# Two orders in a hybrid decoder kernel: DMAs of two groups issued alternately, evictions of product sums handed out unit by unit

## The chip, the core and the metric

The kernel runs on one core of one Trainium2 chip. The core has five engines with an instruction queue each: TensorE (PE in the profile, with PEld for its weight loads), VectorE (DVE), ScalarE (ACT), GpSimd (POOL) and SyncE (SP, which here only issues DMAs). Matmuls write their sums to PSUM, in eight banks; everything else works in SBUF. An engine runs its queue strictly in order and waits on semaphores for the others. The metric is the time of one execution on the device in microseconds; before the change it is 2410.54 us, the median of three runs (2407.71 to 2413.61).

## The reference

One layer of a decoder over a prompt of 2048 tokens and 64 sample tokens, model width 1024, all in float32:

```python
proj = x @ w_in                       # q | f | i | g | B | C | h
o, state = hgrn2(silu(q), log_f, 1 - f, i)          # gated linear recurrence, 4 heads of 128
o = rms_norm(o) * onorm_g * silu(g)
yc = B * conv3(C * h)                 # causal, depthwise
x = layer_norm(ALPHA * x + concat(o, yc) @ w_out)
x = layer_norm(ALPHA * x + relu(x @ w_ff1) ** 2 @ w_ff2)    # w_ff1 1024 x 4096, w_ff2 4096 x 1024
```

It returns the rows of both groups, and the new states of the recurrence and of the convolution.

## The kernel before

**Blocks and stages.** The prompt is worked in four blocks of 512 tokens (`b`); the 64 sample tokens go with the second. A block runs through the input projection (`m1`, `m2`, `m3`, together `main()`), the recurrence (`head`, `chunks`, `out_stages`), the output projection with the first normalisation, the first MLP matmul (`ff1`, `ff1_product`) and the second (the loop over `ff2_units`). The order of all instructions is written out by hand: generators yield between pieces and the loop at line 862 interleaves them, and each engine's queue is simply the order in which the Python code emits.

**Split numbers.** Every float32 operand of the large matmuls is split in a high and a low part, and a product is three matmuls (`mm3`, lines 239 to 241, and `mm3_on`, 245 to 247): high by high, high by low, low by high. For weights ACT makes the high part `wh` (line 203) and DVE the low part `wl` (line 210); for activations `split` makes `h` on ACT (line 164) and `l` on DVE (line 165).

**The weights' pipeline.** All weights are a list of units of 128 x 1024 values. SP loads each to one of three buffers `st` (line 182), ACT and DVE split it into one of four `wh` and four `wl`. `weights(u)` calls `ahead`, which keeps four units split ahead of the one that PE works on. DVE's part of a step is not emitted at once: it goes on the list `later`, and the next `flush()` emits that list, in order. `ahead` begins with such a flush, so what one unit puts on `later` is emitted as the next unit begins.

**Products with fewer multiplications.** Most of the MLP runs as Strassen-like products: seven in place of eight for a chunk of the hidden width (`PRODUCTS`). Some of these take sums of quarters of the weights. The sums are made once, in DRAM: `T1` to `T4` for each of eight chunks, for `w_ff2` in tensors named `T_b` (`quarter2`) and for `w_ff1` in tensors named `T_a` (`quarter1`). `make_sums` (line 341) is a generator that issues these as DMAs from POOL: it goes through eight steps (copy or accumulate), and in each through its chunks, one DMA of 512 KB per `yield`. A step on a chunk reads or adds to what an earlier step on the same chunk has written, so POOL waits for that DMA to land before it issues. `making` (line 356) first makes the `T_b` sums of chunks 0 to 3 and then the `T_a` sums of chunks 4 to 7, 32 DMAs each. In the first block, from the seventh piece of `main()` on, lines 868 and 869 take two DMAs of it per piece; `hold` (line 351) is a tiny POOL operation that keeps POOL from starting earlier. Further sums come from `making1` during the MLP. POOL also computes the powers of the normalisations: line 720 for the recurrence's output, line 271 for the layer norms.

**The recurrence's output.** `out_stages` (line 711) squares and sums a chunk's heads on ACT (716), adds a constant on DVE (719), takes the power on POOL (720), scales on ACT (723), multiplies by the gate on DVE (725), transposes on PE (729) and splits. Each stage is emitted in a step of its own, between pieces of the projection.

**The second MLP matmul.** A block has two passes (`pl["parts"]`), each over four chunks (three in the last pass of the last block, whose eighth chunk is done apart). A pass runs through the seven products in order, and each product through its chunks: 28 units, each 12 matmuls of 512 columns. A product's sum stands in two PSUM banks (128 rows each): bank pair `D` takes `T4`, `A` takes `B11`, then `T2`, then `T3` on top, `C` takes `B21`, `B` takes `T1` and then `B22`. After a product's last chunk (`c == clast`) the sums are added to rows of the output `x1` in SBUF by `add_to` (line 1238), one DVE operation on 128 x 512 values for each bank and target: two for most products, four for `T3`. The first addition to a target is line 1245, the others are line 1242. These are the evictions. Line 1234, by way of `sum_rows`, makes sums of hidden rows for three of the products; `prepare` splits the hidden rows of the unit two ahead (`h`, `l`). In the second block `sample_sums` adds the sample rows' two half sums (lines 256 and 1252) at once and puts the additions to the output on the list `slow`; each unit moves one entry of `slow` to `later` (line 1307), and what is left is emitted as the pass ends (line 1345).

Of the kernel before, what the change touches and what calls it, by code (L numbers as in the profile page):

```python
# [34 lines left out]
NCH = NF // FC  # L35
# [19 lines left out]
NPART = 4  # L55
# [6 lines left out]
def hybrid_step(ctx, tc, a, o):  # L62
# [45 lines left out]
    def PS(shape=(P, 512)):  # L108
        count[0] += 1
        return psum.tile(list(shape), F32, tag="ps", bufs=8, name=f"ps{count[0]}")  # L110
# [42 lines left out]
    later = []  # L153

    def flush():
        for _ in range(len(later)):
            later.pop(0)()

    def flush_all():
        while later:  # L160
            flush()
# [64 lines left out]
    def weights(i, kept=0):  # L226

        ahead(i + 4 - kept)
        return handles.pop(i)
# [23 lines left out]
    def upper(bank):  # L253

        tmp = TMP().rearrange("p a b -> p (a b)")
        s.activation(tmp[:NS], bank[NS:2 * NS, :], AF.Copy)
        return tmp[:NS]


    def norm_weights(which, rows=range(2)):  # L260

        for i in rows:
            nc.sync.dma_start(lnb[:, i, :], a["lnb"][:, 2 * which + i, :])
# [78 lines left out]
    def make_sums(at, cs):  # L342
        for to, of, acc in (("T1", "B11", False), ("T3", "B22", False), ("T1", "B12", True), ("T3", "B12", True),
                            ("T2", "T3", False), ("T2", "B11", True), ("T4", "T2", False), ("T4", "B21", True)):
            for c in cs:
                if acc:
                    g.dma_start(at(c, to), at(c, of), accum_op=ALU.add, max_dma_last_dim=4096)
                else:
                    g.dma_start(at(c, to), at(c, of), max_dma_last_dim=4096)
                yield  # L350

    def hold(x):

        g.tensor_tensor(tick, x, x, ALU.add)

    making = chain(make_sums(quarter2, range(NPART)), make_sums(quarter1, range(NPART, NCH)))
    making1 = chain(make_sums(quarter2, range(NPART, NCH)), make_sums(quarter1, range(NPLAIN, NPART)))

    for b in range(NB):
# [44 lines left out]
    for b in range(NB):  # L404
# [542 lines left out]
        def drain():  # L947
            while lnq:
                before()
                after()  # L950
                flush()
# [31 lines left out]
        for ps_i, tl in enumerate(pl["tiles"]):  # L983
# [5 lines left out]
            banks = {(t, dh): PS() for t in tl for dh in range(2)}  # L989
# [45 lines left out]
        def values(c):  # L1035
            if c not in raw:

                raw[c] = F((P, 4, 2, 256), "raw", NPART)
            return raw[c]
# [170 lines left out]
        def prepare():  # L1210
            if not queue:
                return
            step, c = queue.pop(0)
            r = raw[c]
            x = r[:, SLOT_OF[step]]
            h, l = F((P, 2, 256), "h", 3, F32R), F((P, 2, 256), "l", 3, F32R)
            split(h, l, x)
            hid[step, c] = (h, l)
            if step in SUMMED:
                assert (step, c) in summed  # L1220
            seen.add((step, c))
            if step == PRODUCTS[-1][0]:
                del raw[c]
# [14 lines left out]
        def add_to(t, dh, bank, sign):  # L1238
            z = x1[t][:, dh * 512:dh * 512 + 512]
            op = ALU.add if sign > 0 else ALU.subtract  # L1240
            if (t, dh) in touched:
                v.tensor_tensor(z, z, bank, op)
            else:
                touched.add((t, dh))
                v.scalar_tensor_tensor(z, z, ALPHA, bank, ALU.mult, op)

        slow = []

        def sample_sums(bank, into):

            up = upper(bank)
            v.tensor_tensor(up, up, bank[:NS, :], ALU.add)

            def add(dh, sign):
                z = x1[NC][:NS, dh * 512:dh * 512 + 512]
                op = ALU.add if sign > 0 else ALU.subtract
                if (NC, dh) in touched:
                    v.tensor_tensor(z, z, up, op)
                else:
                    touched.add((NC, dh))  # L1260
                    v.scalar_tensor_tensor(z, z, ALPHA, up, ALU.mult, op)

            for dh, sign in into:
                slow.append(lambda dh=dh, sign=sign: add(dh, sign))

        for part, (ff1_units, ff2_units) in enumerate(pl["parts"]):
            queue += [(step, c) for step, c, _ in ff2_units]
            for i, (step, c, u) in enumerate(ff1_units):
                if part == 1 and i in (4, 12):
                    norm_weights(1, (i // 8,))  # L1270
                if len(ff1_units) - 5 <= i < len(ff1_units) - 3:
                    prepare()
                if b == 0 and part == 0:
                    if i == 0:
                        for _ in making:
                            pass
                    ff1(step, weights(u), segs)
                    hold(values(c)[:, 0, 0, 0:1])
                    next(making1, 0)
                    next(making1, 0)  # L1280
                else:
                    ff1_product(step, c, weights(u))
                    if b == 0 and i < 8:
                        hold(values(c)[:, 0, 0, 0:1])
                        next(making1, 0)
            drain()
            if part == 1:
                xq.clear()
            sumq += [(k, c) for k in SUMMED for c in sorted({c for _, c, _ in ff2_units})]
            nsum = 0  # L1290
            spairs = []
            squeue = [c * FC + 2 * SAMPLE[step][0] for step, c, _ in ff2_units if samp and step in SAMPLE]

            def sample_rows():
                if squeue:
                    f = squeue.pop(0)
                    hp = F((P, 2, P), "hp", 2, F32R)
                    split(hp[:, :, 0:NS], hp[:, :, NS:P], sample_values(f // FC, f))
                    spairs.append(hp)

            banks = {}
            sample_rows()
            cfirst, clast = ff2_units[0][1], ff2_units[-1][1]
            for n_, (step, c, u) in enumerate(ff2_units):
                w = weights(u)
                if slow:
                    later.append(slow.pop(0))
                while sumq and (nsum * 3 + 6) // 2 <= n_:
                    sum_rows()
                    nsum += 1  # L1310
                parts = [tuple(x[:, q * 512:q * 512 + 512] for x in w) for q in range(2)]
                prepare()
                if step in SAMPLE:
                    sample_rows()
                if pl["last"] and step == PRODUCTS[-1][0] and c >= NCH - 3:
                    if c == NCH - 3:
                        last = [F((P, 4, 2, 256), "raw", NPART, F32R) for _ in range(2)]
                    for x in ((0, 2), (1, 3))[c - NCH + 3]:
                        split(last[0][:, x], last[1][:, x], raw[NCH - 1][:, x])
                k = to[step]  # L1320
                first = k not in banks
                if first:
                    banks[k] = [PS() for _ in range(2)]
                h, l = hid.pop((step, c))
                if b == 0 and n_ % 3 == 0:
                    hold(h[:, 0, 0:1].bitcast(F32))
                    next(making1, 0)
                for p in range(2):
                    cs = slice(p * P, p * P + P)
                    for q, (rh, rl) in enumerate(parts):  # L1330
                        mm3_on(banks[k][p], h[:, q, cs], l[:, q, cs], rh, rl, first and q == 0, c == clast and q == 1)
                if samp and step in SAMPLE:
                    if c == cfirst:
                        ys = PS()
                    hp = spairs.pop(0)
                    for q, (rh, rl) in enumerate(parts):
                        mm_pair(ys, hp[:, q, :], rh, rl, c == cfirst and q == 0, c == clast and q == 1)
                if c == clast:
                    for t0, dh, sign in INTO[k][step]:
                        for p in range(2):  # L1340
                            add_to(t0 + p, dh, banks[k][p], sign)
                    if samp and step in SAMPLE:
                        sample_sums(ys, SAMPLE[step][1])
            while slow:
                slow.pop(0)()

# [138 lines left out]
```

## Time and profile before

| what | value |
|---|---|
| median of three runs | 2410.54 us |
| the profiled execution | 2411.07 us, span 2409.3 us |
| mean granted clock of TensorE | 0.993 |
| DMA traffic of the POOL queue | 67.71 MB, 11.5% of 16 engines' span |
| DMA traffic of the SP queue | 347.96 MB, 45.0% |
| evictions at lines 1242 and 1245 | 104 and 32, 686 and 687 ns each (medians) |
| `wl` at line 210 | 580, 1221 ns each |

The span is that of the instructions; the execution has 1.8 us around it. Rows of the timeline give start, duration, engine, line, operation, output <- inputs, shapes and, in brackets, how long the engine stood idle before the row and what ended that. Rows of the waits give who waited for whom, the sum in us, how often, and the longest. POOL's rows `DMA_DIRECT2D` are the issue of a DMA, not its transfer.

### The profile page before, as it was taken

What the parts mean: (1) busy time and instruction counts of PE and PEld (TensorE: products, weight loads), DVE (VectorE), ACT (ScalarE), POOL (GpSimd) and SP (SyncE); (2) the same over time, 40 slices, a digit from 0 to 9 for tenths busy, and PEclk for the clock granted to TensorE, in tenths of its full rate; (3) what the DMA queues carried; (4) which work ended last, traced back from release to release, by engine and by line L of the source; (5) the groups of instructions that cost most, each with busy time, mean ns of one, the idle gap of its engine ahead of it and who ended that gap; (6) DMA issues with size and microseconds to landing.
All of it is one profiled execution on the core that took longest, in us unless ns stands there. A gap on an engine that the chain in (4) does not pass through costs nothing.

```text
span 2409.3 us, 38088 instructions
## 1 busy us (share of the span) xinstructions
PE 2343.9 (97%) x15036; PEld 2041.3 (85%) x15036; DVE 1788.1 (74%) x2832; ACT 1233.7 (51%) x1922; POOL 188.9 (8%) x244
## 2 busy tenths in 40 slices
PE   8988999999999999999999999999999999999998
PEld 7777987887979889979978788998988778998996
DVE  7845858568786567885688966888588974888578
ACT  5224645565423546655754334665665324565563
POOL 2321021101100200000000000000000001000001
PEclk9998999999999999999999999999999999999999
DMA  8997588868523454545554325456575225456653
GB/s 278 285 255 193 157 244 272 260 210 239 155 87 90 130 159 140 166 146 178 177 173 123 101 71 186 155 184 193 194 215 167 97 80 171 142 176 199 196 189 123
DMA packets 131507, 418.89 MB, mean 174 GB/s; under 512 B 13376, under 2 KB 17856, under 8 KB 131328
## 3 DMA queue, kind: packets, MB, share of 16 engines
q1 hardware_dynamic: 108880, 347.96, 45.0%
q0 software_dynamic: 22016, 67.71, 11.5%
q8 instruction: 118, 1.93, 0.3%
q10 hardware_dynamic: 432, 0.79, 0.1%
q14 instruction: 61, 0.50, 0.1%
HBM read 405.36 MB, written 69.77 MB: 197 GB/s over the span
## 4 chain that ended last, share of the span: by engine, by line
PE 51%; DVE 5%; issue 1%; ACT 0%; DMA 0%; POOL 0%; POOLq 0%; DVEq 0%; ACTq 0%
PE ps L247 10%; PE ps L245 9%; PE ps L246 9%; PE ps L239 6%; PE ps L241 6%; PE ps L240 6%; DVE wl L210 1%; PE ps L250 1%; PE ps L251 1%; PE ps L683 1%; DVE l L165 0%; DVE S L603 0%; DMA st<-in_w_ff 0%; DVE S L693 0%; PE ps L777 0%
## 5 line engine op out<-in xcount | busy, mean ns | idle before, releaser
L210 DVE TENSOR_TENSOR wl<-st,wh 128x1024 fp32r<-128x1024 f32 x580 | 707.6, 1221 | 159.4 <-ACT wh L203 158.1
L203 ACT ACTIVATE wh<-st 128x1024 fp32r<-128x1024 f32 x581 | 613.6, 1056 | 376.2 <-DMA st<-in_w_ff 89.5
L239 PE MATMUL ps<-X,wh 128*128 128x256 f32 (+2 forms) x1376 | 465.4, 338 | 10.0 <-ACT X L164 8.5
L240 PE MATMUL ps<-X,wh 128*128 128x256 f32 (+2 forms) x1376 | 455.7, 331 | 0.3 <-DVE X L165 0.3
L241 PE MATMUL ps<-X,wl 128*128 128x256 f32 (+2 forms) x1376 | 455.2, 331 | 0.0
L247 PE MATMUL ps<-wh,l 128*128 128x512 f32 x868 | 343.5, 396 | 14.1 <-DVE l L165 13.8
L245 PE MATMUL ps<-wh,h 128*128 128x512 f32 x868 | 339.6, 391 | 3.2 <-ACT h L164 3.2
L246 PE MATMUL ps<-wl,h 128*128 128x512 f32 x868 | 339.2, 391 | 0.0
L239 PEld LDWEIGHTS ps<-X,wh 128*128 128x128 f32 x1376 | 262.3, 191 | 34.5 <-ACT X L164 8.7
L241 PEld LDWEIGHTS ps<-X,wl 128*128 128x128 f32 x1376 | 262.0, 190 | 22.0
L240 PEld LDWEIGHTS ps<-X,wh 128*128 128x128 f32 x1376 | 262.4, 191 | 20.9 <-DVE X L165 1.0
L247 PEld LDWEIGHTS ps<-wh,l 128*128 128x128 f32 x868 | 163.7, 189 | 63.4 <-DVE l L165 30.1
L245 PEld LDWEIGHTS ps<-wh,h 128*128 128x128 f32 x868 | 163.7, 189 | 36.4 <-ACT h L164 4.0
L246 PEld LDWEIGHTS ps<-wl,h 128*128 128x128 f32 x868 | 163.7, 189 | 34.3
L165 DVE TENSOR_TENSOR l<-raw,h 128x512 fp32r<-128x512 f32 x217 | 148.8, 686 | 9.7 <-ACT h L164 9.7
L245 PE MATMUL ps<-X,wh 128*128 128x256 f32 (+1 forms) x528 | 152.0, 288 | 1.8 <-ACT wh L203 1.8
L247 PE MATMUL ps<-X,wl 128*128 128x256 f32 (+1 forms) x528 | 152.1, 288 | 1.4 <-DVE wl L210 1.4
L246 PE MATMUL ps<-X,wh 128*128 128x256 f32 (+1 forms) x528 | 151.9, 288 | 0.0
L271 POOL TENSOR_TENSOR sm<-sm,nhalf 128x1 f32<-128x1 f32 (+1 forms) x34 | 34.6, 1017 | 1342.2 <-DVE sm L270 1296.0
L1147 DVE TENSOR_TENSOR raw<-raw,ps 128x512 f32<-128x512 f32 (+1 forms) x112 | 61.0, 571 | 102.4 <-PE ps L247 102.3
L164 ACT ACTIVATE h<-raw 128x512 fp32r<-128x512 f32 x217 | 134.0, 617 | 1.6 <-PE ps L246 1.6
L239 PE MATMUL ps<-wh,X 128*128 128x512 f32 x256 | 105.5, 412 | 2.8 <-DVE S L603 2.8
(259 smaller groups left out, 4372.3 us busy)
## 6 DMA issues: line engine op xcount, KB each, us to landing
st<-in_w_ff SPq DMA_DIRECT2D x227, 512.0 KB, 3.7
st<-T_b SPq DMA_DIRECT2D x124, 512.0 KB, 3.8
st<-in_w_in SPq DMA_DIRECT2D x110, 512.0 KB, 3.7
st<-T_a SPq DMA_DIRECT2D x88, 512.0 KB, 3.5
st<-in_w_out SPq DMA_DIRECT2D x56, 512.0 KB, 4.5
T_b<-in_w_ff POOLq DMA_DIRECT2D x48, 512.0 KB, 11.5
T_a<-in_w_ff POOLq DMA_DIRECT2D x36, 512.0 KB, 12.3
T_b<-T_b POOLq DMA_DIRECT2D x16, 512.0 KB, 8.7
```

The lines of the kernel that those rows point to most:

```text
L164: s.activation(hi, src, AF.Copy)
L165: later.append(lambda: v.tensor_tensor(lo, src, hi.bitcast(F32), ALU.subtract))
L203: s.activation(wh, st, AF.Copy)
L210: v.tensor_tensor(wl, st, wh.bitcast(F32), ALU.subtract)
L239: te.matmul(out, lh, rh, start=first, stop=False)
L240: te.matmul(out, lh, rl, start=False, stop=False)
L241: te.matmul(out, ll, rh, start=False, stop=last)
L245: te.matmul(out, lh, rh, start=first, stop=False, skip_group_check=True)
L246: te.matmul(out, lh, rl, start=False, stop=False, skip_group_check=True)
L247: te.matmul(out, ll, rh, start=False, stop=last, skip_group_check=True)
L271: g.tensor_tensor(st[:n, 15:16], st[:n, 14:15], nhalf[:n, 0:1], ALU.pow)
L1147: v.tensor_tensor(z, z, ps, (ALU.add, ALU.subtract)[op - 2])
```

## The change

Three edits. The generator `making` takes one DMA of the `T_b` group and one of the `T_a` group in turn (each `next` of the pair's first half issues both, that of its second half none), in place of all of one group and then all of the other. At the end of a product the evictions go on the list `slow` in place of being emitted at once; each unit then moves one entry of `slow` to `later`, or two while there are more than four. As a pass ends, `later` is emitted in full before the entries still on `slow`.

```diff
-    making = chain(make_sums(quarter2, range(NPART)), make_sums(quarter1, range(NPART, NCH)))
+    making = (None for pair in zip(make_sums(quarter2, range(NPART)), make_sums(quarter1, range(NPART, NCH))) for _ in pair)
...
                 w = weights(u)
-                if slow:
-                    later.append(slow.pop(0))
+                for _ in range(2 if len(slow) > 4 else 1):
+                    if slow:
+                        later.append(slow.pop(0))
...
                 if c == clast:
                     for t0, dh, sign in INTO[k][step]:
                         for p in range(2):
-                            add_to(t0 + p, dh, banks[k][p], sign)
+                            slow.append(lambda z=(t0 + p, dh, banks[k][p], sign): add_to(*z))
                     if samp and step in SAMPLE:
                         sample_sums(ys, SAMPLE[step][1])
+            flush_all()
             while slow:
                 slow.pop(0)()
```

## The prediction

> **What bounds the kernel now.** I read the page first: the span and the first part say which engine fills it.
>
> ```profile
> span 2409.3 us, 38088 instructions
> PE 2343.9 (97%) x15036; PEld 2041.3 (85%) x15036; DVE 1788.1 (74%) x2832; ACT 1233.7 (51%) x1922; POOL 188.9 (8%) x244
> ```
>
> TensorE (PE) is busy for 2343.9 of 2409.3 us, so neither part of the change can win more than the 65.4 us in which it stands. The second view, the waits of PE, says on whom it waits there (total, times, longest):
>
> ```profile
> PE ps L729 <- DVE S L725: 16.6, 2, 14.0
> PE ps L247 <- DVE l L165: 13.8, 17, 1.7
> PE ps L245 <- ACT h L164: 3.2, 2, 1.9
> PE ps L250 <- DVE hp L165: 2.6, 2, 1.3
> ```
>
> The reader is to see two kinds of loss: one place with 16.6 us in two waits (the transposes of line 729 in the first block), and many short waits for `l`, `h` and `hp`, the split hidden values of the second MLP matmul, together 19.6 us. The third view, the timeline around the long wait, first on PE, then on ACT, DVE and POOL:
>
> ```profile
> 165.02 0.48 PE L239 MATMUL ps<-X,wh 128*128 128x512 f32 x1
> ...
> 167.84 0.38 PE L774 MATMUL ps<-tok,S 128*128 128x128 f32 x2
> ...
> 172.13 0.39 PE L241 MATMUL ps<-X,wl 128*128 128x512 f32 x1
> 186.51 1.12 PE L729 MATMUL ps<-ident,S 128*128 128x128 f32 x4 [13.99 <-DVE S L725]
> 190.20 1.12 PE L729 MATMUL ps<-ident,S 128*128 128x128 f32 x4 [2.57 <-DVE S L725]
> 190.97 0.78 PE L239 MATMUL ps<-X,wh 128*128 128x512 f32 x1
> ...
> 194.82 0.60 PE L729 MATMUL ps<-ident,S 128*128 128x128 f32 x4
> ```
>
> ```profile
> 184.59 1.14 ACT L723 ACTIVATE S<-ps,sm 128x128 f32<-128x128 f32 x4 [21.71 <-POOL sm L720]
> ```
>
> ```profile
> 161.96 0.17 DVE L719 TENSOR_SCALAR sm<-sm 128x4 f32<-128x4 f32 x1 [3.22 <-ACT S L716]
> ...
> 185.76 0.69 DVE L725 TENSOR_TENSOR S<-S,tok 128x512 f32<-128x512 f32 x1 [16.83 <-ACT S L723]
> ```
>
> ```profile
> 179.18 4.29 POOL L347 DMA_DIRECT2D T_a<-in_w_ff  x4 [1.40 <-DMA T_a<-T_a]
> 182.84 2.69 POOL L720 TENSOR_TENSOR sm<-sm,nhalf 128x4 f32<-128x4 f32 x2
> ```
>
> Read backwards: PE waits for DVE line 725, DVE for ACT line 723, ACT for POOL line 720, the tiny power of two chunks. Its input was ready at 161.96, and the row of 182.84 has no bracket: POOL waited for no data, it was late. All 64 DMAs of `making` stand ahead of it in POOL's queue, and each issue waits for an earlier one to land. So in this stage POOL's queue of accumulating DMAs is the bound.
>
> **Part one, the DMA order.** It adds no DMA, removes none and moves none past another engine's instruction: at each place two `next(making)` still issue two. Only the order inside the 64 differs. A step needs the step before it of the same chunk; within one group of four chunks that is 4 DMAs back, with the groups alternating it is 8 back. What decides is when the last DMA can be issued. First, is the transfer side full?
>
> ```profile
> 30.00:35.00 5.00, 5.00 (x24) 4.11 (x23) 1.78 (x4) 3.32 (x6) 2.53 (x3) 1.00 1.01 364
> 35.00:40.00 5.00, 5.00 (x24) 4.10 (x23) 4.96 (x9) 2.93 (x5) 1.94 (x3) 1.00 1.04 400
> ...
> 180.00:185.00 5.00, 0.00 (x0) 0.00 (x0) 0.00 (x0) 0.41 (x2) 5.00 (x6) 0.50 0.91 159
> ...
> 190.00:195.00 5.00, 4.80 (x18) 4.01 (x19) 0.92 (x3) 3.44 (x11) 1.01 (x1) 0.68 0.95 193
> 195.00:200.00 5.00, 5.00 (x27) 4.16 (x26) 4.97 (x8) 2.67 (x4) 0.00 (x0) 1.00 0.47 107
> ```
>
> The columns are the stretch, its length, busy time of PE, PEld, DVE, ACT, POOL, PE's clock, the DMA share and GB/s. The share is 0.91 or more in all 33 stretches from 30 to 195 and 0.47 in the next: the queue runs full and is through at about 195 + 0.47 x 5 = 197.4. A full queue isn't shortened by another order, so I keep 197.4 as its end. What changes is how much is already issued by then. The price of an accumulating transfer is read where a copy waits for each of four in turn (first and last of four, twice):
>
> ```profile
> 78.50 0.54 POOL L349 DMA_DIRECT2D T_b<-T_b  x1 [2.47 <-DMA T_b<-in_w_ff]
> ...
> 89.57 0.52 POOL L349 DMA_DIRECT2D T_b<-T_b  x1 [3.27 <-DMA T_b<-in_w_ff]
> ...
> 167.81 0.55 POOL L349 DMA_DIRECT2D T_a<-T_a  x1 [2.26 <-DMA T_a<-in_w_ff]
> ...
> 177.27 0.52 POOL L349 DMA_DIRECT2D T_a<-T_a  x1 [2.08 <-DMA T_a<-in_w_ff]
> ```
>
> (89.57 - 78.50) / 3 = 3.69 us for a `T_b`, (177.27 - 167.81) / 3 = 3.15 for a `T_a`. After the change the last eight DMAs are four of each, 4 x 3.69 + 4 x 3.15 = 27.4 us, and the last of them is issued once the copy eight back has landed: 197.4 - 27.4 = 170.0. From the other side: now the last copy has landed when the row of 179.18 issues its last, about 182.3 (183.47 less one issue of 1.1), and with the four last `T_b` transfers behind it that becomes 182.3 - 14.8 = 167.5. I take the middle, 168.8, plus 1.1 for the issue: the power starts at about 169.5 to 170 (taken: 169.5), in place of 182.84, 13.3 us earlier. The transposes follow it by 186.51 - 182.84 = 3.67 and 190.20 - 182.84 = 7.36, so at 173.2 and 176.9; PE is free at 172.5, so some 3 us of the wait stay: ACT's and DVE's chain to the second transpose is what is late next. With the shorter wait the clock need not fall: the twelve matmuls from 190.97 to 194.82 took 3.85 us against 2.82 from 165.02 to 167.84, and each group of four transposes 1.12 against 0.60; 1.0 of the first and 0.5 of the second I count as won. **Part one: -13.3 - 1.5 = -14.8 us.** Bounds: not above 16.6 + 2.1 = 18.7 (both waits and all slow clock gone), not below 0 (power still at 182.84).
>
> What moves later is the `T_b` sums, complete near 197 and not before the first `T_a`; nothing reads them before the first block's second MLP matmul. The loads of weights run beside a queue that is as full now.
>
> [...]
>
> **Part two, the evictions.** Count and kind stay: 16 per pass, eight passes. Now they stand in DVE's queue right after their product; DVE meets them before PE is done, waits, and runs two or four in a row. The end of one pass shows it, with the waits of DVE over the whole run:
>
> ```profile
> DVE tok L1242 <- PE ps L247: 39.7, 51, 2.7
> DVE tok L1245 <- PE ps L247: 16.6, 26, 1.5
> ```
>
> ```profile
> 1666.31 0.69 DVE L1242 TENSOR_TENSOR tok<-tok,ps 128x512 f32<-128x512 f32 x1 [0.61 <-PE ps L247]
> 1667.67 1.88 DVE L1242 TENSOR_TENSOR tok<-tok,ps 128x512 f32<-128x512 f32 x3 [0.67 <-PE ps L247]
> 1669.47 1.22 DVE L210 TENSOR_TENSOR wl<-st,wh 128x1024 fp32r<-128x1024 f32 x1
> 1670.61 0.69 DVE L165 TENSOR_TENSOR l<-raw,h 128x512 fp32r<-128x512 f32 x1
> ```
>
> ```profile
> 1671.35 0.50 PE L247 MATMUL ps<-wh,l 128*128 128x512 f32 x1 [0.54 <-DVE l L165]
> ```
>
> Behind them come the unit's `wl` and `l`, for which PE then stands 0.54. Afterwards one eviction (two while more than four are left) goes into `later` per unit and so between a unit's `wl` and its `l`. The new wait is for a product that ended a unit or more ago; `wl` ahead of it already needs a buffer that PE frees no earlier, so it should wait for nothing; behind it stand `l` and the next `wl`, and for these PE and ACT. A unit of PE is twice 1667.67 - 1666.31, 2.72 us. On DVE it holds `wl` 1.14 (1670.61 - 1669.47), `l` 0.60, in two of three units up to the 20th a sum of 0.60, and now an eviction of 0.60: 2.94 at the worst, 0.22 too much, in five units of a pass by the order of the code, and the 56.3 us above are DVE's to spend.
>
> What is won, by pass (the waits of PE for `l` in the windows of both passes of the first block, the second of the third, and one of those with a single wait):
>
> ```profile
> PE ps L247 <- DVE l L165: 3.5, 5, 1.1
> PE ps L247 <- DVE l L165: 5.1, 4, 1.7
> PE ps L247 <- DVE l L165: 2.3, 3, 1.1
> PE ps L247 <- DVE l L165: 0.5, 1, 0.5
> ```
>
> First block 3.5 and 5.1 (and 3.2 for `h`, where ACT waits for loads beside accumulating DMAs: not won); second block: its two waits for `hp`, 1.3 each, are not won, since there the sample rows' sum at line 1252 still stands at once and waits for PE; third 0.5 and 2.3, fourth 0.5 and 0.5. The possible sum is 3.5 + 5.1 + 0.5 + 2.3 + 0.5 + 0.5 = 12.4. The four-in-a-row waits I count whole; those in the first block are half due to late loads, and what a moved 0.60 costs a unit later comes off: I take half, **-6.5 us**; bounds -12.4 and, with five units of 0.22 in each of eight passes and nothing won, +8.8. The flush added at a pass's end brings the next unit's `wl` ahead of the last evictions: nothing, hidden by four units of weights ahead.
>
> **The sum.** The profiled execution took 2411.07 us (span 2409.3 and 1.8 around it): 2411.1 - 14.8 - 6.5 = 2389.8. It lies 0.5 above the median 2410.54, so **2389.3** against the median.
>
> **The rivals.** (a) *The relief is partial*: `T_a` and `T_b` transfers slow each other, the power starts near 176. Against it, the 1.0 share at all times; for it, that no stretch of before alternates. 2410.5 - 7.8 - 6.5 = 2396. (b) *The evictions only move the waits*: `l` is late a unit later, because `wl`, sum, eviction and `l` fill 2.94 of 2.72 us. For it, DVE's own load; against it, the 56.3 us. 2410.5 - 14.8 = 2396. (c) *The chain shortens*: with more in flight the queue itself ends earlier and the long wait goes whole: 2410.5 - 18.7 - 6.5 = 2385. Against it, the share. [...] (d) *The new order doesn't free the power*: POOL is through at 182.8 as before, because eight in flight slow what was four: 2410.5 - 6.5 = 2404. (e) *Slower*: an eviction in front of `l` costs PE its whole 0.60. There are 128 spread ones; with 64 such, 38.4 us, against 14.8 and 12.4 won: 2422. It decides from (14.8 + 12.4) / 0.60 = 45 of them on. Against it: DVE reaches most `l` early enough, since only 17 waits for one are seen.
>
> **How the numbers follow.** Chances: forecast 0.60, (a) 0.12, (b) 0.14, (c) 0.05, (d) 0.05, (e) 0.04. The forecast's own width, from the power at 167 to 173 and evictions at 2 to 11, is 2382 to 2396; with (a), (b) and (c) the range 2381 to 2399 leaves out (d), (e) and the wider misses of the two terms. A difference of under 0.2% (4.8 us) can't be told from none here: faster 0.90 (all but (e), a part of (d) and some of the slack of (b)), same 0.06, slower 0.04.
>
> **What would show it.** Right: in POOL's timeline `T_b` and `T_a` alternate, the last issue and line 720 stand near 170, PE's wait at line 729 is about 3 us in sum and no clock of 0.5 follows; DVE's waits for PE at lines 1242 and 1245 fall from 56.3 to under 20; no row of four evictions, no wait of 0.54 in the last two blocks. Wrong: line 720 still behind 180, or many more waits of PE for `l`, or loads of weights that land too late between 170 and 200.

## The result, and the profile after

| | before | after |
|---|---|---|
| median of five runs each | 2410.96 us | 2396.96 us |
| lowest to highest | 2407.71 to 2413.61 | 2392.39 to 2405.57 |
| span of the profiled execution | 2409.3 us | 2394.7 us |

The ratio is 0.9948, with a 95% interval of 0.9925 to 0.9971: faster by 14.0 us, where 21.3 were forecast. The page of the profile of after:

```profile
span 2394.7 us, 38161 instructions
PE 2343.2 (98%) x15036; PEld 2043.5 (85%) x15036; DVE 1785.2 (75%) x2832; ACT 1232.0 (51%) x1922; POOL 197.4 (8%) x244
```

PE's busy time is nearly as before (2343.2 against 2343.9), so all but 0.7 of the 14.6 us by which the span is shorter are idle time. The waits of PE over the whole run say which idle time:

```profile
PE ps L247 <- DVE l L165: 11.6, 17, 1.8
...
PE ps L245 <- ACT h L164: 4.1, 3, 2.5
...
PE ps L729 <- DVE S L725: 3.3, 2, 3.0
PE ps L250 <- DVE hp L165: 3.2, 3, 1.3
```

The long wait at line 729 fell from 16.6 to 3.3. The waits for `l`, `h` and `hp`, which the second part of the change is about, were 19.6 together and are 18.9: their sum has hardly moved. The two parts are now read one after the other.

**The DMA order.** POOL's timeline of after, up to the late power, and PE's timeline around the transposes:

```profile
152.04 0.52 POOL L349 DMA_DIRECT2D T_b<-T_b  x1 [2.41 <-DMA T_b<-in_w_ff]
155.62 0.52 POOL L349 DMA_DIRECT2D T_a<-T_a  x1 [3.06 <-DMA T_a<-in_w_ff]
...
167.72 0.82 POOL L347 DMA_DIRECT2D T_b<-in_w_ff  x1 [0.23 <-DMA T_b<-T_b]
168.97 1.05 POOL L347 DMA_DIRECT2D T_a<-in_w_ff  x1 [0.43 <-DMA T_a<-T_a]
169.56 2.53 POOL L720 TENSOR_TENSOR sm<-sm,nhalf 128x4 f32<-128x4 f32 x2
```

```profile
173.07 0.66 PE L729 MATMUL ps<-ident,S 128*128 128x128 f32 x4 [0.24 <-DVE S L725]
176.76 1.11 PE L729 MATMUL ps<-ident,S 128*128 128x128 f32 x4 [3.04 <-DVE S L725]
177.53 0.78 PE L239 MATMUL ps<-X,wh 128*128 128x512 f32 x1
...
181.55 0.60 PE L729 MATMUL ps<-ident,S 128*128 128x128 f32 x4
```

`T_b` and `T_a` alternate, the last issue stands at 168.97, the power starts at 169.56 in place of 182.84, and the third group of transposes at 181.55 in place of 194.82: 13.3 us earlier. The twelve matmuls from 177.53 on still run slowly: 4.02 us up to the third group, as against 3.85 before. From the end of the second wait on the granted clock is 0.50 for 3.4 us:

```profile
176.60:180.00 3.40, 3.24 (x10) 2.76 (x11) 0.88 (x3) 3.39 (x11) 1.01 (x1) 0.50 1.06 229
```

The transfers that POOL issued also end sooner, on which the forecast did not count: from 190 to 195 they take 73.8% of the 16 DMA engines' time before and 12.4% after, and their last packet ends at 198.1 before and at 194.2 after.

**The evictions.** The 56.3 us of waits of DVE at lines 1242 and 1245 for PE's line 247 are gone from the list of waits. Here are DVE's waits in the window of the second block's passes (1000 to 1310), first of before, then of after, and behind them a stretch of DVE's timeline of after in the third block:

```profile
DVE tok L1242 <- PE ps L247: 15.7, 15, 2.7
DVE tmp L1252 <- ACT tmp L256: 6.8, 8, 0.8
DVE tok L1245 <- PE ps L247: 6.2, 7, 1.5
```

```profile
DVE tmp L1252 <- ACT tmp L256: 32.5, 8, 5.0
```

```profile
1646.96 1.23 DVE L210 TENSOR_TENSOR wl<-st,wh 128x1024 fp32r<-128x1024 f32 x1 [0.29 <-ACT wh L203]
1648.10 0.68 DVE L1245 SCALAR_TENSOR_TENSOR tok<-tok,ps 128x512 f32<-128x512 f32 x1
1648.70 0.69 DVE L165 TENSOR_TENSOR l<-raw,h 128x512 fp32r<-128x512 f32 x1
1649.68 1.23 DVE L210 TENSOR_TENSOR wl<-st,wh 128x1024 fp32r<-128x1024 f32 x1 [0.30 <-ACT wh L203]
```

The timeline is what the change is meant to make: one eviction between `wl` and `l`, waiting for nothing, and 0.3 us of DVE to spare in that unit of 2.72 us, which holds no sum of rows. In the second block it is otherwise. Before, DVE waited 15.7 + 6.2 + 6.8 = 28.7 us there for products; now it waits 32.5 for them, all at line 1252, the half sum of the sample rows. That one still stands at once at the product's end, and what is saved at the evictions is waited for there.

Stage by stage, the change of the idle and slow time is worked out by taking the same matmul of the program in both traces: how much earlier or later it starts after than before, and by how much that changes across the stage (us, negative is a gain):

| stage (time in before) | change |
|---|---|
| the late power, 172 to 200 | -13.6 |
| first block, two passes | -1.4 and +1.9 |
| second block, two passes | +0.8 and +1.8 |
| third block, two passes | -1.3 and -0.6 |
| fourth block, two passes | -1.8 and -0.4 |

The last eight entries are the second part of the change, with whatever chance is in them: -1.0 us in sum. It wins 4.1 in the last two blocks and loses 2.6 in the second. Between the stages of the table two larger differences nearly cancel: -1.4 between the first block's passes and the second's, where before has a drop of the clock at 923.6 (0.51 for 3.4 us) and after has none, and +1.0 between the second block's and the third's, where before has a drop of 3.4 us at 1357.1 (0.51) and after one of 6.8 us at 1344.0 (0.50).

### The profile page after: what moved, and what is told of

Same layout as the page of the kernel before. It is cut to its first block, busy times and chain, and to the rows that moved or that the text cites. A ratio compares the mean times of both kernels' runs of the same rounds, so it can differ in the third digit from the quotient of the medians.

```text
span 2394.7 us, 38161 instructions
## 1 busy us (share of the span) xinstructions
PE 2343.2 (98%) x15036; PEld 2043.5 (85%) x15036; DVE 1785.2 (75%) x2832; ACT 1232.0 (51%) x1922; POOL 197.4 (8%) x244
## 4 chain that ended last, share of the span: by engine, by line
PE 49%; DVE 6%; issue 1%; DMA 1%; ACT 1%; POOL 0%; POOLq 0%; DVEq 0%; ACTq 0%
PE ps L247 9%; PE ps L245 9%; PE ps L246 9%; PE ps L239 6%; PE ps L241 6%; PE ps L240 6%; DVE wl L210 1%; DMA st<-in_w_ff 1%; PE ps L250 1%; PE ps L683 1%; DMA st<-in_xt 1%; PE ps L251 1%; DVE l L165 0%; DVE S L603 0%; ACT wh L203 0%
```

## The experiments

In the edits below `-` is the kernel after the change and `+` the experiment, unless another base is named. "Stage change" always means the comparison just described, against the profiled execution of before, so each is a difference of two single executions; on the chips of the experiments before took a median of 2412.84 us (`e1` to `e4`), 2410.18 (`e5` to `e8`), 2414.13 (`e9`, `e10`) and 2413.92 (`e11`).

### The two parts alone

`e1_order_only` takes back the evictions, `e2_evict_only` the order of the DMAs.

```diff
 e1
-                for _ in range(2 if len(slow) > 4 else 1):
-                    if slow:
-                        later.append(slow.pop(0))
+                if slow:
+                    later.append(slow.pop(0))
...
-                            slow.append(lambda z=(t0 + p, dh, banks[k][p], sign): add_to(*z))
+                            add_to(t0 + p, dh, banks[k][p], sign)
...
-            flush_all()
 e2
-    making = (None for pair in zip(make_sums(quarter2, range(NPART)), make_sums(quarter1, range(NPART, NCH))) for _ in pair)
+    making = chain(make_sums(quarter2, range(NPART)), make_sums(quarter1, range(NPART, NCH)))
```

> Only the order of the 64 DMAs is changed; the evictions stand as before. Theory: the order is worth what the trace of the changed kernel shows where PE leaves the long wait, 13.4 us, so the span is about 2409.3 - 13.4 = 2396, the ratio near 0.9945, and PE's waits at line 729 are 3 us in sum. Rival (the order only pays together with the evictions, for instance because the sums' DMAs and the late loads of the first block's MLP hang together): 5 us or more of it is given back before the second block, and the span is above 2400.

> Only the evictions are handed out unit by unit; the DMAs stand in the old order. Theory: they are worth the rest, about 1 us of span (2408 to 2409), within what a measurement can't tell from nothing: waits of PE behind four evictions in a row go (4 us in the third and fourth block), and the second block gives back about 2.5. Rival (the prediction's term was right and the profiled execution is an unlucky one): 5 to 8 us, a span of 2402 to 2404.

`e1` took 2399.56 us, 0.994 [0.9921, 0.9958]; `e2` took 2411.86, 0.9992 [0.9978, 1.0006]. The order alone gives the whole gain within the intervals; the evictions alone give 1.0 us in the median, and the interval holds no change at all. That the order's gain is the long wait is seen in the waits of PE of `e1`: 5.0 us of the 16.6 at line 729 are left, and the stage change there is -11.2, with -13.6 in the change itself. Both transposes waited in this execution (2.0 and 3.0); in that of after the first waited only 0.24. The span of this execution is 2401.0, on the rival's side of 2400. It stands 3.2 above the median run, and it has 3.5 us more than before between the first block's two passes, a stretch that differs by -0.5 to +3.6 over the runs, in kernels of both orders; so it is no sign that the order pays only with the evictions.

Six of the kernels have the same code up to this stage's end (after, `e1`, `e3`, `e5`, `e7`, `e8`). In their profiled executions the power starts between 168.48 and 171.50, and the stage change lies between -11.0 and -13.9: the execution of after is one of the better ones.

### What the second block gives back

`e3_second_block_at_once` spreads the evictions in all blocks but the second; `e8_sample_sum_later` goes the other way and puts the half sum of line 1252 on the list `slow` too, ahead of the additions that read it.

```diff
 e3
-                            slow.append(lambda z=(t0 + p, dh, banks[k][p], sign): add_to(*z))
+                            z = (t0 + p, dh, banks[k][p], sign)
+                            if samp:
+                                add_to(*z)
+                            else:
+                                slow.append(lambda z=z: add_to(*z))
 e8
-            up = upper(bank)
-            v.tensor_tensor(up, up, bank[:NS, :], ALU.add)
+            half = []
+            def both():
+                up = upper(bank)
+                v.tensor_tensor(up, up, bank[:NS, :], ALU.add)
+                half.append(up)
+            slow.append(both)
...
+                up = half[0]
```

> The changed kernel, but in the second block, the one with the sample rows, the evictions are emitted at once as before. Theory: the loss of the second block comes from evictions that now stand between a unit's wl and its l and hp while DVE still waits for the sample rows' half sums (line 1252), so the span falls by 2 to 3 us, to about 2392, and the extra waits of 0.57 for l in the second block go. Rival (the loss there is the chance of this execution, or comes from the flush at the pass's end): no difference, 2394 to 2395, with the same waits.

> The changed kernel, but the sum of the sample rows' halves (lines 256 and 1252) goes on the same list behind the evictions, so that DVE and ACT no longer wait for PE at the end of those products. Theory: this wait (32.5 us of DVE in eight times) is what makes hp and l late in the second block, so the seven waits of PE there (5.0 us in sum, at hp 1.31 and at l 0.57) fall to under 1.5 and the span by 4 to 5 us, to about 2390. Rival (DVE has too much work in a unit of the second block, whatever waits): the waits only move, and the span stays within 1 us of 2394.7.

`e3` took 2397.29, 0.9933 [0.9915, 0.995], an interval that overlaps that of the change; `e8` took 2389.98, 0.9907 [0.9893, 0.9922]. The waits of PE in the window of the second block's passes (990 to 1300), in the kernel after and in `e8`:

```profile
PE ps L250 <- DVE hp L165: 3.2, 3, 1.3
PE ps L247 <- DVE l L165: 2.3, 4, 0.6
```

```profile
PE ps L250 <- DVE hp L165: 0.6, 1, 0.6
```

The stage change of the two passes is +2.6 in the change, +0.7 with the second block's evictions at once, and -5.6 with the half sum spread as well. The sizes repeat: +2.3 to +2.6 in the five kernels that spread the evictions and keep the half sum at once (after, `e2`, `e4`, `e6`, `e7`), 0.0 to +0.7 in the four with that block's evictions at once (`e1`, `e3`, `e10`, `e11`), and -5.6 and -5.5 in the two that spread both (`e8`, `e9`). So spread evictions lose here only while the half sum keeps its place and its wait. DVE's timeline of after shows the cost, `wl` and `l` of the unit emitted behind 4.38 us of waiting:

```profile
1054.46 0.68 DVE L1252 TENSOR_TENSOR tmp<-tmp,ps 64x512 f32<-64x512 f32 x1 [4.38 <-ACT tmp L256]
1055.07 1.21 DVE L210 TENSOR_TENSOR wl<-st,wh 128x1024 fp32r<-128x1024 f32 x1
...
1056.81 0.68 DVE L165 TENSOR_TENSOR l<-raw,h 128x512 fp32r<-128x512 f32 x1
```

In `e8`, where the half sum is line 1255 of the kernel, DVE waits for it 1.4 us in all, in place of 32.5 (window 1000 to 1310):

```profile
DVE tmp L1255 <- ACT tmp L256: 1.4, 3, 0.7
```

The edit of `e8` puts off ACT's half of the sum too. At line 256 ACT waited for PE for 17.2 us before and 17.3 after, and waits 5.6 in `e8` (990 to 1300). So ACT's wait is not what the change made worse, but how much of the gain of `e8` is ACT's was not separated, and no run spreads the half sum with the evictions at once.

### Only the fours spread

`e5_four_only` spreads the evictions of the products with more than one target, and emits the pairs at once.

```diff
-                            slow.append(lambda z=(t0 + p, dh, banks[k][p], sign): add_to(*z))
+                            z = (t0 + p, dh, banks[k][p], sign)
+                            if len(INTO[k][step]) > 1:
+                                slow.append(lambda z=z: add_to(*z))
+                            else:
+                                add_to(*z)
```

> The new DMA order, and of the evictions only the four of T3 are handed out unit by unit; those of the other products, two each, are emitted at once as before. Theory: only four in a row make PE wait (0.54 each time, about 0.9 with the restart), and handing out the twos buys nothing and costs new waits in units that hold a sum too; so the third and fourth block lose none of their gain (about 4 us against the order alone), the second block gives nothing back, and the span is near 2391 to 2392. Rival (the twos carry the gain, too): the span is above 2394, with more waits of PE for l in the third and fourth block than the full change has there (3).

It took 2398.03, 0.9946 [0.9933, 0.9958], no better than the change. The stage change of the last two blocks is -1.8 where the change has -4.1. The theory that the rows of four carry the gain, drawn from the wait of 0.54 behind such a row, fell: the pairs carry about half. Part of that half is behind the last pass, where PE waits 1.1 us for `wl` in `e5` and 0.3 in the kernel after.

### The rest of the wait at line 729

About 3 us of wait and a slow clock were left in that stage. `e4_last_eight_behind` issues the last eight DMAs of `making` behind all four powers of the block, `e6_behind_two_powers` behind the first two (where `i`, the count of pieces of `main()`, is 46).

```diff
 e4
-                next(making, 0)
-                next(making, 0)
+                if i < 6 + 28:
+                    next(making, 0)
+                    next(making, 0)
...
+        if b == 0:
+            for _ in making:
+                pass
 e6
-                next(making, 0)
-                next(making, 0)
+                for _ in range(2 if i < 34 else 8 * (i == 46)):
+                    next(making, 0)
```

> The changed kernel, but the last eight of the 64 DMAs are issued after the last piece of the input projection, behind the four powers of line 720. Theory: POOL's place in its queue and not the amount of data is what PE waited for, so the powers start when their inputs are ready, near 158 and 162, PE's waits at line 729 fall from 3.3 us to under 0.5, and the span falls by about 3 us, to 2391.5. Rival (ACT or DVE are what is late at the second transpose, whatever POOL does): the wait of 3.0 us stays and the span with it.

> The changed kernel, but the last eight of the 64 DMAs stand in POOL's queue right behind the first two powers of line 720, so that they are issued at 162 and not at 157 to 170 and still find the queue full. Theory: the wait at line 729 goes whole, as in the run with the eight at the end of the projection, and since the transfers end no later than now (about 195) the loads behind them are not late: no wait at line 239 near 204, a span 3 to 4 us below that of the changed kernel, near 2391. Rival (the loads' lateness comes from PE being earlier, not from the transfers being later): the wait of 2.65 us for wh near 204 shows here too, and the span stays near 2393 to 2395.

`e4` took 2396.2, 0.9932 [0.9912, 0.9951]; `e6` 2389.63, 0.9909 [0.9895, 0.9923]. In both the wait at line 729 is gone and the stage change is -18.7, all that the stage had to give. `e4` gives 5.6 of it back right behind, which neither its theory nor its rival had. Its POOL timeline, its waits of PE from 165 to 215 and its stretch from 200 to 205, with the same stretch of after behind it, show why:

```profile
173.49 0.88 POOL L347 DMA_DIRECT2D T_b<-in_w_ff  x1
...
177.37 3.86 POOL L347 DMA_DIRECT2D T_a<-in_w_ff  x1
```

```profile
PE ps L239 <- ACT wh L203: 2.7, 1, 2.7
PE ps L240 <- DVE wl L210: 0.8, 1, 0.8
```

```profile
200.00:205.00 5.00, 1.83 (x7) 0.94 (x5) 1.04 (x1) 1.06 (x1) 0.00 (x0) 1.00 1.06 286
```

```profile
200.00:205.00 5.00, 5.00 (x24) 4.14 (x23) 3.89 (x4) 2.91 (x4) 0.00 (x0) 1.00 0.51 141
```

The eight accumulations are issued in a burst from 173.49 on, and the DMA share is still 1.06 from 200 to 205, where it is 0.51 in the kernel after. PE waits 2.7 us for `wh` and 0.8 for `wl` of the next projection; that the loads of weights behind them come through late is inferred from the share. In `e6` the burst begins at 163.00, the remaining two powers stand behind it and still in time, and from 165 to 215 PE waits for nothing:

```profile
162.04 1.02 POOL L720 TENSOR_TENSOR sm<-sm,nhalf 128x4 f32<-128x4 f32 x1 [2.56 <-DVE S L532]
163.00 0.89 POOL L347 DMA_DIRECT2D T_b<-in_w_ff  x1
...
169.52 2.59 POOL L720 TENSOR_TENSOR sm<-sm,nhalf 128x4 f32<-128x4 f32 x1
```

Is the alternation needed then, or would it have been enough to move the DMAs behind two powers? `e11_old_order_behind_powers` makes the edit of `e6` on the kernel before.

> The kernel before, with its groups one after the other and its evictions at once; only the last eight of the 64 DMAs (four copies and four accumulations of T_a) stand behind the first two powers of line 720. Theory: the alternation helps only by letting POOL issue earlier, so a queue that lets the powers pass does the same without it: the 56th DMA is issued near 164.5, the powers follow at 165.6 where they stood at 182.8, the wait at line 729 falls from 16.6 us to under 1, and the span by 17 to 18, to about 2391.5. Rival (the alternation also feeds the transfers better, so that without it the last copies and sums come late and the loads of weights behind them too): the gain at line 729 is given back by waits for wh behind 195, and the span stays above 2395.

It took 2407.65, 0.9966 [0.995, 0.9982]: above 2395, as the rival has it, but not for the rival's reason: most of the gain at line 729 did not come, and none of it is given back to waits for `wh` there. POOL's timeline and the wait of PE:

```profile
163.04 2.50 POOL L720 TENSOR_TENSOR sm<-sm,nhalf 128x4 f32<-128x4 f32 x2
...
182.63 1.03 POOL L347 DMA_DIRECT2D T_a<-in_w_ff  x1 [0.23 <-DMA T_a<-T_a]
183.21 2.50 POOL L720 TENSOR_TENSOR sm<-sm,nhalf 128x4 f32<-128x4 f32 x2
```

```profile
PE ps L729 <- DVE S L725: 9.8, 1, 9.8
```

The first two powers are on time at 163.04, but the four `T_a` copies and four accumulations behind them still wait for landings, four DMAs back, the last until 182.63, and the next powers stand behind those. One late power has become another: the stage change is -7.1 in place of -18.7. So the alternation is what lets POOL get through its queue by 170. The place of the powers is worth 7.1 us without the alternation, and the last 5 us with it.

### The first block

In the second pass of the first block `making1` issues further sums from POOL while the units run. `e7_sums_out_of_second_pass` issues those in the second block's projection instead.

```diff
-            if b == 1 and i % 2 == 0:
+            if b == 1 and i >= 24:
                 next(making1, 0)
...
-                if b == 0 and n_ % 3 == 0:
+                if b == 0 and part == 0 and n_ % 3 == 0:
```

> The changed kernel, but no accumulating DMA is issued beside the second pass of the first block; the ten that stood there go to the second block's input projection. Theory: the waits of that pass (8.2 us in seven, between 518 and 592) come from loads of weights that land late beside the accumulating transfers, so no order of the evictions could win them; without these transfers they fall to 2 us or less, and the span falls by 6 to 7 us, unless the second block pays for the ten. Rival (DVE's own load makes l late there): the waits stay at 6 us or more.

It took 2388.61, 0.9906 [0.9892, 0.9919]. The waits of PE in that pass (490 to 600), the DMA issues (size, median us to landing) and the stretch from 500 to 605, first of after, then of `e7`:

```profile
PE ps L247 <- DVE l L165: 4.3, 5, 1.8
PE ps L245 <- ACT h L164: 4.1, 3, 2.5
```

```profile
st<-in_w_ff SPq DMA_DIRECT2D x12, 512.0 KB, 5.3
T_a<-in_w_ff POOLq DMA_DIRECT2D x8, 512.0 KB, 8.0
```

```profile
500.00:605.00 105.00, 96.32 (x438) 78.30 (x438) 80.72 (x104) 54.53 (x70) 19.14 (x22) 0.95 0.78 231
```

```profile
PE ps L247 <- DVE l L165: 1.9, 3, 1.1
```

```profile
st<-in_w_ff SPq DMA_DIRECT2D x13, 512.0 KB, 4.2
```

```profile
500.00:605.00 105.00, 103.11 (x533) 87.81 (x532) 84.53 (x108) 61.78 (x82) 2.11 (x2) 1.00 0.63 196
```

With the sums out of the pass, the eight accumulating DMAs of POOL are gone, the loads of weights from `w_ff` land in 4.2 us in place of 5.3, the waits fall from 8.4 to 1.9, the clock stays at 1.00, and the stage change is -10.5 (+1.9 in the change). ACT's waits for loads from `w_ff` in this window fall with them, from 21.7 us (the longest 4.3) to 11.3 (1.6): `h` and `l` were late behind late weights. The second block's projection, which now has the sums beside it, shows no price: the stretch between the first block's passes and the second's has +0.1, and +0.1 in `e1` and `e6`, which leave the sums where they were. The evictions were not what PE waited for here.

### All of it

`e9_all_four` is the change with the edits of `e6`, `e7` and `e8`; `e10_without_evictions` has the order and the edits of `e6` and `e7`, with all evictions at once.

> The changed kernel with the three edits that each won something: the last eight DMAs behind the first two powers, no accumulating DMA beside the first block's second pass, the sample rows' half sums on the list. Theory: the losses lie in different stages and on PE alone, so the gains add up: 14.6 (the change) + 5 (rest of the wait at line 729) + 10 (second pass of the first block) + 8 (second block) = 37 to 39 us, a span of 2370 to 2372, a ratio near 0.984. Rival (they share one slack, for instance DVE's or the queue's): under 30 us, a span above 2379.

> The same without any change to the evictions: new DMA order, last eight behind the first two powers, no accumulating DMA beside the first block's second pass; evictions and the sample rows' sums at once as before. It prices the handing out where loads are on time. Theory: it wins about 1 us in each pass without sample rows and, with the half sums put off too, 2 to 3 in each of the second block's, so this kernel stands 10 to 13 us behind the one with all four, at 2381 to 2385, and the second pass of the first block shows waits for l again behind T3. Rival (late loads were all of it, the evictions nothing outside the second block): 6 us or less behind.

`e9` took 2374.74, 0.9843 [0.9821, 0.9866], and beats both kernels: 39.4 us under before on the same chip. `e10` took 2383.79, 0.9881 [0.986, 0.9901]; each of its four runs is slower than each of the five of `e9`. The difference of 9.05 us, a little under the 10 to 13 expected, is what spreading the evictions and the half sum together is worth: the stage changes of the second, third and fourth block are together -9.2 in `e9` and +0.1 in `e10`, and that of the first block's second pass is -10.4 and -10.5, the same with and without spreading; the waits for `l` that were expected there behind `T3` are 1.7 us in both. The profiled execution of `e9` (span 2376.3) is above what was expected of it, by stretches of slow clock that the last section takes up.

## Why the prediction was right, and where it was off

**What bounds the kernel, right.** POOL's queue of accumulating DMAs set the long wait: its order alone moved the time by as much as the change within the intervals (`e1`), and the power's start moved with the last issue. The time alone would not show it: 2396.96 is also what rivals (a) and (b) give, 2396 each, and it takes the traces to tell them from the forecast.

**Part one, -13.3, right to a few tenths.** Power at 169.5 forecast and 169.56 found; transposes at 173.2 and 176.9 forecast, 173.07 and 176.76 found; some 3 us of wait forecast, 3.04 found. The last issue, taken at 168.8 between two estimates, stands at 168.97. (168.8 and the 1.1 of the issue are 169.9, not the 169.5 taken; the power starts 0.59 after the last issue, whose row is 1.05 long: the two rows overlap.) There is luck in this. The first estimate took the end of the transfers from before, on the ground that another order doesn't shorten a full queue, which was the author's assumption and is shown by no row of before, as 197.4, of which 27.4 us were the last eight. The last packet ends at 194.2, and the last accumulation, which had waited for the copy eight back, is issued at 168.97, so the last eight take some 25.2: the two errors, 3.2 and 2.2, go opposite ways. And the power's start differs between executions, 168.48 to 171.50 over six kernels with this code. The term for the clock, -1.5, was wrong: after the remaining 3 us of wait the clock fell again (0.50 from 176.60 to 180.00), the twelve matmuls took 4.02 us, and only the first transposes got faster (0.66 in place of 1.12). With 13.6 us in the stage, part one was forecast 1.2 too large; with the -11.0 to -13.9 of the six kernels, 0.9 to 3.8.

**Part two, -6.5, is the step that failed.** The waits were counted by whom the view names, `l` on DVE, and half of 12.4 us was taken (half of 12.4 is 6.2; the text has 6.5). In the change the eight passes bring -1.0. Two things in that step were wrong:

- *The first block's half, 4.3 us, was not there.* The prediction put half of its 8.6 us down to late loads. In the second pass it is all of it: spreading makes no difference once the sums are moved (-10.4 and -10.5 in `e9` and `e10`) and wins nothing before (+1.9 in the change, -0.4 in `e1`), while moving the sums makes 10.5. For the first pass no run took the loads away, and the stage changes (-1.4 in the change, -0.4 in `e2`) are within what executions differ by.
- *The second block was counted at 0 and lost 2.6.* The prediction saw that line 1252 still stands at once, and drew from it only that nothing is won. DVE's waiting moved there whole, 6.8 to 32.5 us, and with evictions now between a unit's `wl` and `l` the work behind it came later than before. `e8`, which puts the half sum off too, turns the +2.6 into -5.6.

In the last two blocks the step was too careful: 3.8 possible, half taken, and 4.1 measured (3.2 to 4.6 over the kernels that spread all evictions there, -0.5 to +0.8 us of change in the three that spread none). The forecast gain of 21.3 less these 5.5 and the 1.2 of part one leaves 14.6, the difference of the spans; the medians differ by 14.0.

**The rivals.** The partial relief (a) and the rival that the order doesn't free the power (d) fell with the power's start. (The 7.8 in the sum of (a) isn't worked out; a power at 176 is 6.8 earlier than 182.84.) That the evictions only move the waits (b) is what happened in the second block, though not by the mechanism given: DVE was not too full, one immediate wait was left. (c) came half true: the transfers do end earlier (194.2 against 198.1; 192.8 to 195.5 over the six kernels), but 3.3 us of the wait stayed, and for that to go whole it needed the place of the last eight (`e4`, `e6`). (e), slower by 0.60 for each eviction in front of `l`, did not appear: where nothing else stands in the way the spread evictions win.

## What to carry to other kernels

Where an engine issues DMAs that wait for each other, interleave independent chains so that a dependency is more issues back (eight in place of four here, and the power 13.3 us earlier), and look at which small operations stand behind them in the same queue: the place of eight issues was worth 5 us too, and a burst too late (`e4`) cost 5.6. Before moving an operation off a wait, ask which wait stays in the same queue and will collect what is saved; spreading most of them and leaving one lost 2.6 us where spreading the last one as well, on both engines that work on it, won 5.6. A wait "for `l`" beside a busy DMA queue may be a wait for weights: in the pass of `e7` the waits fell from 8.4 to 1.9 us with the transfers gone, so take them away before blaming the engine named.

## What the hardware did that was not expected

**The clock fell after two short waits in one execution, and not after the same two in another.** At one place of the fourth block PE waits twice, for 1.39 and 1.34 us. PE's timeline of before and of `e5`, and behind them a stretch of 6.8 and of 6.9 us around the second wait, of the same two:

```profile
1915.71 0.50 PE L239 MATMUL ps<-wh,X 128*128 128x512 f32 x1 [1.39 <-DVE S L603]
...
1918.03 1.07 PE L683 MATMUL ps<-S,S 128*64 128x64 f32 x40 [1.34 <-ACT tok L506]
```

```profile
1901.41 0.50 PE L239 MATMUL ps<-wh,X 128*128 128x512 f32 x1 [1.39 <-DVE S L603]
...
1903.73 1.70 PE L683 MATMUL ps<-S,S 128*64 128x64 f32 x40 [1.34 <-ACT tok L506]
```

```profile
1915.80:1922.60 6.80, 5.46 (x73) 3.97 (x77) 6.71 (x18) 3.77 (x7) 0.57 (x1) 1.00 0.57 219
```

```profile
1902.80:1909.70 6.90, 5.97 (x50) 4.93 (x51) 5.42 (x16) 3.28 (x6) 0.48 (x1) 0.51 0.46 161
```

The waits are the same; the granted clock is 1.00 in the one and 0.51 in the other, and the same 40 small matmuls take 1.07 and 1.70 us. In `e5` the stage around it is 2.6 us longer than before. The profiled execution of `e9` has five such stretches, one of 6.8 us and four of 3.4 at a granted clock of 0.51 to 0.57, of which this is the last:

```profile
1886.00:1889.40 3.40, 3.40 (x44) 2.75 (x43) 3.33 (x11) 1.98 (x4) 0.00 (x0) 0.51 0.59 187
```

That of `e10` has one (its mean granted clock is 0.998, that of `e9` 0.994). In the stretches around them `e9` is 6.9 us behind `e10`, and so the two spans differ by only 4.9 us where the medians differ by 9.05. Waits of 1.39 and 1.34 us, then, were followed by a drop in one execution and by none in another. What decides between the two, and what sets the lengths of 3.4 and 6.8 us, no run shows.

**Left open.** How much of the differences in the first block's first pass, between -2.3 and +2.6 over the runs, is chance was not settled.
